# First FFN weights of block two rounded inside the attention loop, and one group of DRAM adds issued inside the attention's closing

## The chip, the cores and the metric

One core of one Trainium2 chip. The metric is the device time of one execution in microseconds; the kernel before took 1028.0 us (median of 3 runs, 1027.74 to 1028.08). PE is TensorE, DVE is VectorE, ACT is ScalarE, POOL is GpSimd, and SP is SyncE, which here only issues DMA.

## The reference

Two decoder blocks over 512 tokens of width 1024, in fp32: block one is a gated short convolution and a SwiGLU, block two is sliding-window attention with sinks and a SwiGLU.

```
for l in range(DEPTH):                        # DEPTH = 2
    if l < N_A:
        mix = short_conv_mixer(rmsnorm(h, ...), a_w_in[l], a_conv_w[l], a_w_out[l])
        h = h + rmsnorm(mix, a_post_norm[l])
    else:
        ...                                   # shared k, v; q; 16 heads, window 128, sinks
        attn = sliding_window_sink_attention(q, k_sh, v_sh, b_sinks[j]) @ b_w_o[j]
        h = h + rmsnorm(attn, b_post_norm[j])
    ff = swiglu(rmsnorm(h, ffn_pre_norm[l]), ffn_w_gate_up[l], ffn_w_down[l])
    h = h + rmsnorm(ff, ffn_post_norm[l])
```

The place of interest is the middle line of the second branch: the product with `b_w_o`, the norm behind it, and the first product of the SwiGLU that follows.

## The kernel before

Every fp32 operand is split into a high part, rounded to float32r, and a low part, the rest; a product is three matmuls (`mm3`). So each weight tile costs, beside its 512 KB fetch into one of seven `raw` buffers (SP queue, `fetch`), a rounding on ACT (`whi<-raw`) and a subtraction on DVE (`wlo<-raw,whi`). `Ahead` does this for the weights of the next stage: its constructor issues two fetches, and each `one()` rounds one 128x1024 tile, subtracts, and fetches the next.

The large products save multiplications by working with sums of weight blocks. These sums are formed in DRAM by DMA: `Sums` lists the copies and the accumulating transfers, `sum_on(at)` first issues all that is pending on the POOL queue and then makes the next step of every running group pending, and `issue(n)` issues pending ones. A group with four sums has four steps: four copies (`ab`, `ac`, `abc`, `abcd`), then `ab += b` and `ac += c`, then `abc += ab`, then `abcd += abc`. A transfer whose source or destination another transfer is still writing waits on the POOL engine's queue, and what stands behind it there waits too.

The attention loop runs `i` from 0 to 9 (`KT + 2` passes). `ORDER` is the order of one pass, written by hand; each letter is a step for a pair of heads `t` that depends on `i`. In pass 8 only the tail of the last pair, t = 7, is left: its probabilities are transposed (T, tile `pt`), split into `phi` on ACT (P) and `plo` on DVE (L), for the last block into `lp`, and multiplied with the values (W, tile `po`). Beside this, pass 8 holds the last two early units of the output projection (Z into `pe`, copied out by z into `mixo`) and the rounding of the last `w_o` tile (G). Pass 9 holds O, which splits `po` into `ohi` and `olo`.

Then comes `close`, for four token tiles t = 0 to 3 of two halves each. PE multiplies into `pmix`; for each half DVE adds (`take`, `mixo<-pmix,mixo`, L259) and ACT squares with a sum (`square_mix`, L264); then, for the tile, DVE adds up the sums (`mean`, `uv`, L293), POOL raises to the power -0.5 (`ur`, L297), DVE updates `h` (L302), ACT squares `h` (L310), DVE and POOL form the second factor (`mean2`: L315, L319), and ACT writes the normed tile (`norm`, `xn`, L324). In the middle of the last half tile (3, 1) PE transposes `xn` of tiles 0 and 1 (`turn`, tile `xt`, L335). Behind it, `ffn(1)` begins with `last_tile` and `project_first` (tile `pgu`). The first half tiles of `close` are begun in two parts of nine matmuls each, with two `ahead.one()` behind each part.

On PE, DVE, ACT and POOL the order of the instructions is that of the code (`manual_schedule`); on SP the scheduler orders the transfers.

Of the kernel before, what the change touches and what calls it, by code (L numbers as in the profile page):

```python
# [19 lines left out]
KT = D // P  # L20
# [24 lines left out]

EARLY_IN, REST_IN = 2, 0
ORDER = (
    "R- T0 g0 S0 O- T1 Q0 M0 Q1 Z0 P0 P1 S1 T2 L0 Q2 L1 G M1 E00 E01 T3 H- Q3 P2 P3 E10 E11 Z1 z0 K W0 L2 L3 N0 W1 W2 N1 W3 g1 z1"
)
STEP = {  # L50
    "S": "scores", "M": "maxima", "E": "exponents", "N": "normalise", "T": "turn", "P": "high",
# [4 lines left out]
EARLY = 4  # L56
# [8 lines left out]
G_FPRE = (24, 32)  # L65
# [3 lines left out]
B_CONV, B_ATT, B_FFN = 0, 1, (2, 3)  # L69
# [3 lines left out]
def yoco_kernel(  # L73
# [54 lines left out]
    def bank(s, pool=None):  # L128

        if pool is None:  # L130
            pool = (ps_mm, ps_sc, ps_mm, ps_pt)[turn[0] % 4]
            turn[0] += 1
        return pool.tile([P, S], F32, tag="bank", name=name(s))
# [69 lines left out]
    def unit(ps, t, ws, x, ks, n, k0=0, c0=0, c1=S):  # L203

        tk = slice(t * P, (t + 1) * P)
        for k in ks:
            w = ws[k // 2]
            kk = slice((k % 2) * S + c0, (k % 2) * S + c1)
            mm3(ps, x[k0 + k][0][:, tk], x[k0 + k][1][:, tk], w[0][:, kk], w[1][:, kk],
                k == 0, k == n - 1)  # L210
# [313 lines left out]
    issues = []  # L524

    def issue(n, behind=None):

        for dst, src, op in issues[:n]:
            if len(dst.shape) == 3:
                dst, src = (t.rearrange("k (a b) c -> (k a) (b c)", b=4) for t in (dst, src))  # L530
            else:
                dst, src = (t.rearrange("(a b) c -> a (b c)", b=2) for t in (dst, src))
            kw = {} if op is None else {"accum_op": op}
            made = tc.keep_in_program_order(
                nc.gpsimd.dma_start(dst, src, max_dma_last_dim=4 * 4 * S, **kw))  # L535
            if behind is not None:
                tc.add_manual_dep(
                    made.ins, behind.ins.name, mybir.DependencyInfo(
                        mybir.DependencyClass.Sync, mybir.DependencyReason.DATA),
                    reason="pace")  # L540
        del issues[:n]
# [13 lines left out]
    def sum_on(at):  # L555

        issue(len(issues))
        if at in BEGIN:
            summing.append(sums_of[BEGIN[at]])
        for x in summing:  # L560
            x.step()
        summing[:] = [x for x in summing if x.steps]
# [164 lines left out]
    res = Update(mix_c, B_CONV, [G_FPRE[0]])  # L727
# [116 lines left out]
    def tile_done(res, t, square=True):  # L844

        if t > 0:
            res.mean2(t - 1)
        res.scale(t, 0)
        res.mean(t)
        if t > 0:  # L850
            res.norm(t - 1)
        res.scale(t, 1)
        res.update(t)
        if square:
            res.square(t)

    def close(ws, x, k0, res, ahead, then=None):


        n = len(x) - k0  # L860

        def part(ps, t, half, ks):
            unit(ps, t, ws[len(ws) // 2 * half :], x, ks, n, k0)

        begun = [bank("pmix", ps_mm) for _ in range(2)]
        for half in range(2):
            part(begun[half], 0, half, range(n - 1))
            ahead.one()
            ahead.one()
        for t in range(NB):  # L870
            for half in range(2):
                if t == 0:
                    ps = begun[half]
                    part(ps, t, half, range(n - 1, n))
                else:
                    ps = bank("pmix", ps_mm)
                    if (t, half) == (NB - 1, 1):
                        part(ps, t, half, range(2))
                        for b in range(4):
                            res.turn(b, (0, 1))  # L880
                        part(ps, t, half, range(2, n))
                        for f in range(4):
                            res.split(0, f, 0)
                        res.square_mix(t, 0)
                        res.square(NB - 2)
                        res.scale(t, 0)
                    else:
                        part(ps, t, half, range(n))
                res.take(t, half, ps)
                if (t, half) != (NB - 1, 0):  # L890
                    res.square_mix(t, half)
            if t < NB - 1:
                tile_done(res, t, square=t < NB - 2)
            if t == 0 and then:
                then()
# [40 lines left out]
    def first_weights(l):  # L936
        return ([w_gu[l, f, j] for f in range(2) for j in range(2)]
                + [w_gb[l, 0, b] for b in range(2)])
# [3 lines left out]
    ahead = Ahead(first_weights(0))  # L942
    with tc.manual_schedule(engines=ALL):

        def sums_on():
            sum_on("o1")
            issue(len(issues))

        close(ws, ys, 0, res, ahead, sums_on)


    def ffn(l, before, ahead, gain, gpres, following):
# [199 lines left out]
        if gpres:  # L1152
            ahead = Ahead(following)
            with tc.manual_schedule(engines=ALL):
                close(ws, acts[-1], 0, res, ahead)
            return res, ahead
# [29 lines left out]
    res, ahead = ffn(0, res, ahead, B_FFN[0], [G_KV, G_BPRE], [  # L1186
        w_k[0], w_k[1], w_v[:, 0:D], w_v[:, D:], w_q[0], w_q[1]])
# [21 lines left out]
    def rope(ps, eng):  # L1209
        sh = slot("sh")  # L1210
        nc.vector.stream_shuffle(sh, ps, swap)
        a = slot("ra")
        nc.vector.tensor_tensor(out=a, in0=ps, in1=ctab, op=ALU.mult)
        eng.tensor_tensor(out=sh, in0=sh, in1=stab, op=ALU.mult)
        eng.tensor_tensor(out=a, in0=a, in1=sh, op=ALU.add)
        return a

    def rope_split(a, eng):
        hi, lo = slot("rhi", F32R), slot("rlo", F32R)
        nc.scalar.activation(hi, a, AF.Copy)  # L1220
        eng.tensor_tensor(out=lo, in0=a, in1=hi.bitcast(F32), op=ALU.subtract)
        return hi, lo
# [162 lines left out]
    mix_o = [None] * NB  # L1385
    early_w, rest_w = [], []
# [3 lines left out]
    at = []  # L1390

    with tc.manual_schedule(engines=ALL):
        last_tile(res, [[(0, 4)], [(0, 5)], [], [(0, 6), (0, 7), (1, 0), (1, 1)],
                        [(1, f) for f in (4, 5, 2, 3, 6, 7)]])
        for hf in range(2):
            c = slice(hf * 256, (hf + 1) * 256)
# [48 lines left out]
    with tc.manual_schedule(engines=ALL):  # L1445
        sum_on("a0")
        for i in range(KT + 2):
            for c in ORDER.split():
                if c == "K":
                    if i == 2:  # L1450
                        ks.append(rope_split(rope(pk[1], nc.gpsimd), nc.gpsimd))
                    continue
                late = c.endswith("-")
                op, n = c[0], [int(d) for d in c[1:].rstrip("-")]
                t = i - late
                if op == "g":

                    u = 2 * (t - EARLY - 1) + n[0]
                    if u in (-2, -1, 2, 3):
                        j = u + 2 if u < 0 else u  # L1460
                        early_w.append(split_weights(w_o[j // 2, j % 2], slots=j >= EARLY_IN))
                    continue
                if op in "SMENTPLWO":
                    t -= op in "TPLWO"
                    of = hp
                elif op in "QRH":
                    t += LEAD
                    of = qs
                elif op == "G":
                    t += LEAD + 1  # L1470
                    of = qs
                    if KT <= t < KT + 4:
                        j = t - KT
                        rest_w.append(split_weights(w_o[j // 2, 2 + j % 2], slots=j >= REST_IN))
                else:
                    t = 2 * (t - EARLY - 1) + n.pop(0)
                    of = early
                if 0 <= t < len(of) and not (op in "RH" and t < LEAD - 1):
                    getattr(of[t], STEP[op])(*n)
                if op in "RH":  # L1480
                    issue(len(issues) // 2 if op == "R" else len(issues))
            sum_on(f"a{i + 1}")

        res = Update(mix_o, B_ATT, [G_FPRE[1]])
        res.leaves = True
        res.load()
        ahead = Ahead(first_weights(1))
        close(rest_w, at, EARLY, res, ahead)
    ffn(1, res, ahead, B_FFN[1], [], [])


# [93 lines left out]
```

## Time and profile before

| | |
|---|---|
| median of 3 runs | 1028.0 us (1027.74 to 1028.08) |
| the profiled execution: its time | 1032.36 us |
| the profiled execution: its span | 1030.6 us |
| granted TensorE clock, mean over the span | 0.997 |
| busy: DVE | 823.2 us (80%) |
| busy: ACT | 577.7 us (56%) |
| busy: POOL | 195.3 us (19%) |
| the attention's pass 8 and 9 | about 651 to 662 us of the span |
| the closing behind the attention | about 661.5 to 690 us |

The profiled execution is 4.4 us longer than the median of the others, so a difference between two kernels is taken between figures of the same kind. Times in the profile are microseconds from the start of the span. A timeline row gives start, duration, engine, line, operation, the tile written and those read, the count, and in square brackets how long the engine had been idle before it and what ended that. Successive instructions of an engine overlap somewhat, so the pitch of a chain (start to start) is shorter than the duration of one. For a DMA row on POOL the duration is that of the issue; the time until the data has landed is given in the view of the DMA issues.

### The profile page before, as it was taken

To read this page: it belongs to the slowest core of one execution; us is meant where nothing else is said; L and a number is where in the kernel's file an instruction comes from. 1 tells how busy PE (TensorE), PEld (TensorE's weight loads), DVE (VectorE), ACT (ScalarE), POOL (GpSimd) and SP (SyncE) were. 2 spreads that over 40 slices of the span, in tenths; PEclk is the share of its full clock that TensorE was granted. 3 is DMA by queue.
4 is the path that set the end of the run, shared out by engine and by line. 5 is a ranking of instruction groups with operands and counts; after the bars stand their busy time and mean duration, and the time that the engine had idled before them with its cause. 6 is when DMAs were issued, how large, how long until landed. Compare 5 with 4: busy or idle time off the path is not lost.

```text
span 1030.6 us, 17465 instructions
## 1 busy us (share of the span) xinstructions
PE 1019.1 (99%) x6648; PEld 927.8 (90%) x6648; DVE 823.2 (80%) x1400; ACT 577.7 (56%) x1035; POOL 195.3 (19%) x259
## 2 busy tenths in 40 slices
PE   9999999999999999999999999989999999999997
PEld 8888888999899898998897888879998999989986
DVE  5766767888688879779869999668886788887786
ACT  7323445865655354656566677667565554645642
POOL 0333033111111111000124653121111010210001
PEclk9999999999999999999999999999999999999999
DMA  9897689459968699778404789865889676988732
GB/s 355 284 261 229 184 254 353 130 169 299 351 229 293 194 314 332 242 232 296 146 21 149 190 273 254 248 223 158 261 287 328 176 252 203 312 296 251 246 136 82
DMA packets 66580, 244.59 MB, mean 237 GB/s; under 512 B 7872, under 2 KB 8384, under 8 KB 54720
## 3 DMA queue, kind: packets, MB, share of 16 engines
q1 hardware_dynamic: 51328, 145.98, 38.4%
q0 software_dynamic: 14592, 96.48, 36.4%
q8 instruction: 52, 0.85, 0.3%
q10 hardware_dynamic: 576, 1.02, 0.3%
q14 instruction: 32, 0.26, 0.1%
HBM read 237.15 MB, written 102.76 MB: 330 GB/s over the span
## 4 chain that ended last, share of the span: by engine, by line
PE 90%; DVE 4%; DMA 3%; ACT 1%; issue 1%; POOL 1%; DVEq 0%; ACTq 0%
PE gx L193 7%; PE gx L192 7%; PE gx L191 7%; PE gz L193 4%; PE gz L192 4%; PE gz L191 4%; PE pcub L192 4%; PE pcub L193 4%; PE pcub L191 4%; PE px L191 4%; PE px L192 4%; PE px L193 4%; PE pmix L192 2%; PE pmix L191 2%; PE pmix L193 2%; DMA hsum<-in_w_gb_dram 2%
## 5 line engine op out<-in xcount | busy, mean ns | idle before, releaser
L467 DVE TENSOR_TENSOR wlo<-raw,whi 128x1024 fp32r<-128x1024 f32 x225 | 275.2, 1227 | 93.3 <-ACT whi L466 93.2
L466 ACT ACTIVATE whi<-raw 128x1024 fp32r<-128x1024 f32 x225 | 234.2, 1049 | 117.5 <-DVE raw L454 20.4
L191 PE MATMUL gx<-xt,whi 128*128 128x256 f32 x480 | 135.8, 283 | 0.0
L192 PE MATMUL gx<-xt,whi 128*128 128x256 f32 x480 | 135.8, 283 | 0.0
L193 PE MATMUL gx<-xt,wlo 128*128 128x256 f32 x480 | 135.8, 283 | 0.0
L191 PEld LDWEIGHTS gx<-xt,whi 128*128 128x128 f32 x480 | 92.2, 192 | 0.0
L192 PEld LDWEIGHTS gx<-xt,whi 128*128 128x128 f32 x480 | 92.2, 192 | 0.0
L193 PEld LDWEIGHTS gx<-xt,wlo 128*128 128x128 f32 x480 | 92.2, 192 | 0.0
L535 POOL DMA_DIRECT2D hsum<-in_w_gb_dram x96 | 63.4, 747 | 143.7 <-ACT whi L466 82.2
L1001 ACT ACTIVATE st<-gx 128x256 f32<-128x256 f32 x80 | 30.6, 385 | 83.5 <-PE gx L193 83.5
L535 POOL DMA_DIRECT2D hsum<-hsum x32 | 25.3, 790 | 262.4 <-ACT whi L466 208.6
L192 PE MATMUL pcub<-xhi,whi 128*128 128x512 f32 x168 | 65.4, 389 | 0.0
L191 PE MATMUL pcub<-xlo,whi 128*128 128x512 f32 x168 | 65.4, 389 | 0.0
L193 PE MATMUL pcub<-xhi,wlo 128*128 128x512 f32 x168 | 65.4, 389 | 0.0
L191 PE MATMUL px<-wlo,ahi 128*128 128x512 f32 x120 | 46.7, 389 | 0.0
L192 PE MATMUL px<-whi,ahi 128*128 128x512 f32 x120 | 46.7, 389 | 0.0
L193 PE MATMUL px<-whi,alo 128*128 128x512 f32 x120 | 46.7, 389 | 0.0
L193 PE MATMUL gx<-xhi,wlo 128*128 128x256 f32 x160 | 45.3, 283 | 0.0
L191 PE MATMUL gy<-xlo,whi 128*128 128x256 f32 x160 | 45.3, 283 | 0.0
L192 PE MATMUL gy<-xhi,whi 128*128 128x256 f32 x160 | 45.3, 283 | 0.0
L193 PE MATMUL gy<-xhi,wlo 128*128 128x256 f32 x160 | 45.3, 283 | 0.0
L191 PE MATMUL gz<-xt,whi 128*128 128x256 f32 x160 | 45.3, 283 | 0.0
(268 smaller groups left out, 3122.5 us busy)
## 6 DMA issues: line engine op xcount, KB each, us to landing
hsum<-in_w_gb_dram POOLq DMA_DIRECT2D x96, 512.0 KB, 7.9
raw<-hsum SPq DMA_DIRECT2D x88, 512.0 KB, 8.2
raw<-in_w_gb_dram SPq DMA_DIRECT2D x60, 512.0 KB, 7.4
hsum<-in_w_dn_dram POOLq DMA_DIRECT2D x36, 512.0 KB, 8.3
raw<-in_w_dn_dram SPq DMA_DIRECT2D x32, 512.0 KB, 7.3
hsum<-hsum POOLq DMA_DIRECT2D x28, 512.0 KB, 5.6
raw<-in_w_in_dram SPq DMA_DIRECT2D x21, 512.0 KB, 7.6
hsum<-in_w_dn_dram POOLq DMA_DIRECT2D x12, 768.0 KB, 12.6
```

Source lines behind the costliest of these rows:

```text
L191: nc.tensor.matmul(out, whi, xlo, start=start, stop=False, **kw)
L192: nc.tensor.matmul(out, whi, xhi, start=False, stop=False, **kw)
L193: nc.tensor.matmul(out, wlo, xhi, start=False, stop=stop, **kw)
L466: self.begun = nc.scalar.activation(hi[:, :n], raw, AF.Copy)
L467: nc.vector.tensor_tensor(out=lo[:, :n], in0=raw, in1=hi[:, :n].bitcast(F32), op=ALU.subtract)
L535: nc.gpsimd.dma_start(dst, src, max_dma_last_dim=4 * 4 * S, **kw))
L1001: nc.scalar.activation(s, x, AF.Copy)
```

## The change

The constructor of the closing's `Update` and of `Ahead` move to the start of pass 8; four steps A are written into `ORDER`, and in pass 8 each is one `ahead.one()`; in `close` the four calls fall away where `ahead` is `None`. The load of the gain vector (`res.load`) moves to the start of pass 9, still ahead of its use. The last `sum_on` of the loop moves from the end of pass 9 to behind the first tile of `close`, and there what it makes pending is issued at once.

```diff
 ORDER = (
-    "R- T0 g0 S0 O- T1 Q0 M0 Q1 Z0 P0 P1 S1 T2 L0 Q2 L1 G M1 E00 E01 T3 H- Q3 P2 P3 E10 E11 Z1 z0 K W0 L2 L3 N0 W1 W2 N1 W3 g1 z1"
+    "R- T0 g0 S0 O- T1 Q0 M0 Q1 Z0 P0 P1 S1 T2 L0 Q2 L1 G A M1 E00 E01 T3 H- Q3 P2 P3 A E10 E11 Z1 z0 K W0 L2 L3 A N0 W1 W2 N1 W3 g1 z1 A"
 )
...
         for half in range(2):
             part(begun[half], 0, half, range(n - 1))
-            ahead.one()
-            ahead.one()
+            if ahead:
+                ahead.one()
+                ahead.one()
...
         for i in range(KT + 2):
+            if i == KT:
+                res = Update(mix_o, B_ATT, [G_FPRE[1]])
+                res.leaves = True
+                ahead = Ahead(first_weights(1))
+            if i == KT + 1:
+                res.load()
             for c in ORDER.split():
+                if c == "A":
+                    if i == KT:
+                        ahead.one()
+                    continue
...
-            sum_on(f"a{i + 1}")
-
-        res = Update(mix_o, B_ATT, [G_FPRE[1]])
-        res.leaves = True
-        res.load()
-        ahead = Ahead(first_weights(1))
-        close(rest_w, at, EARLY, res, ahead)
+            if i < KT + 1:
+                sum_on(f"a{i + 1}")
+
+        def sums_on():
+            sum_on(f"a{KT + 2}")
+            issue(len(issues))
+
+        close(rest_w, at, EARLY, res, None, sums_on)
     ffn(1, res, ahead, B_FFN[1], [], [])
```

No instruction is added or removed. PE's order does not change. On SP the fetch of the last `w_o` tile moves behind the first two fetches of the gate and up weights.

ACT, pass 8 to the closing, before (L180 is the last `w_o` tile, L408 the first FFN weights, 5859 the last transposed block):

```order
L180 ACTIVATE whi_7438<-raw_7435 128x512
L1343 ACTIVATE phi_7431<-pt_7426 128x512
L1343 ACTIVATE lp_5859<-pt_7445 128x2x128
L1382 ACTIVATE mixo_7159<-pe_7411 128x512
L1382 ACTIVATE mixo_7212<-pe_7453 128x512
L1364 ACTIVATE ohi_7496<-po_7467 128x512
L408 ACTIVATE whi_7522<-raw_7507 128x1024
```

and now:

```order
L180 ACTIVATE whi_7445<-raw_7442 128x512
L408 ACTIVATE whi_7452<-raw_7393 128x1024
L1344 ACTIVATE phi_7438<-pt_7433 128x512
L1344 ACTIVATE lp_5859<-pt_7458 128x2x128
L408 ACTIVATE whi_7466<-raw_7395 128x1024
L1383 ACTIVATE mixo_7159<-pe_7418 128x512
L408 ACTIVATE whi_7495<-raw_7456 128x1024
L1383 ACTIVATE mixo_7212<-pe_7472 128x512
L408 ACTIVATE whi_7520<-raw_7470 128x1024
L1365 ACTIVATE ohi_7530<-po_7486 128x512
```

The four roundings, which stood in a row behind `ohi`, now stand between the steps of pass 8; one is ahead of the last `phi`.

DVE at the same place, before (L181 is the last `w_o` tile, L413 the first FFN weights):

```order
L181 TENSOR_TENSOR wlo_7440<-raw_7435,whi_7438 128x512
L1347 TENSOR_TENSOR plo_7432<-pt_7426,phi_7431 128x512
L1347 TENSOR_TENSOR lp_5860<-pt_7445,lp_5859 128x2x128
L1365 TENSOR_TENSOR olo_7497<-po_7467,ohi_7496 128x512
L413 TENSOR_TENSOR wlo_7523<-raw_7507,whi_7522 128x1024
```

and now:

```order
L181 TENSOR_TENSOR wlo_7447<-raw_7442,whi_7445 128x512
L413 TENSOR_TENSOR wlo_7453<-raw_7393,whi_7452 128x1024
L413 TENSOR_TENSOR wlo_7467<-raw_7395,whi_7466 128x1024
L1348 TENSOR_TENSOR plo_7439<-pt_7433,phi_7438 128x512
L1348 TENSOR_TENSOR lp_5860<-pt_7458,lp_5859 128x2x128
L413 TENSOR_TENSOR wlo_7496<-raw_7456,whi_7495 128x1024
L413 TENSOR_TENSOR wlo_7521<-raw_7470,whi_7520 128x1024
L1366 TENSOR_TENSOR olo_7531<-po_7486,ohi_7530 128x512
```

Two of the subtractions stand ahead of the last `plo` and `lp`, and two ahead of `olo`.

POOL, the end of pass 9 and the start of the closing, before (`hsum_208` to `hsum_211` are `ab`, `ac`, `abc` and `abcd` of the group of down weights that was begun last):

```order
L535 DMA hsum_211<-in_w_dn_dram 64x2048
L535 DMA hsum_208<-in_w_dn_dram 64x2048
L535 DMA hsum_209<-in_w_dn_dram 64x2048
L297 TENSOR_TENSOR ur_7503<-uv_7502,mhalf 128x1
L319 TENSOR_TENSOR ur_7503<-uv_7502,mhalf 128x1
L297 TENSOR_TENSOR ur_7503<-uv_7502,mhalf 128x1
```

and now:

```order
L535 DMA hsum_211<-in_w_dn_dram 64x2048
L535 DMA hsum_208<-in_w_dn_dram 64x2048
L535 DMA hsum_209<-in_w_dn_dram 64x2048
L297 TENSOR_TENSOR ur_7392<-uv_7391,mhalf 128x1
L535 DMA hsum_210<-hsum_208 64x2048
L319 TENSOR_TENSOR ur_7392<-uv_7391,mhalf 128x1
L297 TENSOR_TENSOR ur_7392<-uv_7391,mhalf 128x1
```

The transfer `abc += ab` (`hsum_210<-hsum_208`), which stood behind the eighth and last `ur` of the closing, now stands behind the first; what reads `hsum_208` there is written by the second row.

## The prediction

> **What bounds the kernel now.** I read the page's first part, then the waits of PE, then the timeline of each engine from pass 8 to the end of the closing. First the page's line of busy time and PE's waits over the whole span (what waited, for what: us in total, times, longest):
>
> ```profile
> PE 1019.1 (99%) x6648; PEld 927.8 (90%) x6648; DVE 823.2 (80%) x1400; ACT 577.7 (56%) x1035; POOL 195.3 (19%) x259
> ...
> PE xt L335 <- ACT xn L324: 2.7, 1, 2.7
> PE idle L663 <- DVE ones L140: 1.1, 1, 1.1
> PE psc L1273 <- DVE nm L1285: 0.6, 2, 0.3
> ```
>
> PE is the bound nearly everywhere. Of other engines it waits once for 2.7 us, in the very stage that the change touches, and otherwise for 1.7 us in all. No later wait can swallow a delay of PE, so a microsecond that PE gains or loses here reaches the end. Next PE around that wait, and the stretches behind it (bounds; then busy time and count of PE, PEld, DVE, ACT, POOL; granted clock; DMA share; GB/s):
>
> ```profile
> 681.72 0.39 PE L193 MATMUL pmix<-whi,olo 128*128 128x512 f32 x1
> 681.95 0.27 PE L335 MATMUL xt<-ident,xn 128*128 128x128 f32 x1
> 684.90 2.39 PE L335 MATMUL xt<-ident,xn 128*128 128x128 f32 x15 [2.69 <-ACT xn L324]
> ...
> 687.94 0.63 PE L193 MATMUL pmix<-whi,olo 128*128 128x512 f32 x1
> 688.37 0.63 PE L191 MATMUL pmix<-wlo,ohi 128*128 128x512 f32 x1
> ...
> 685.00:687.00 2.00, 2.00 (x16) 2.00 (x16) 1.90 (x3) 1.39 (x3) 0.06 (x1) 0.77 0.11 41
> 687.00:689.00 2.00, 2.00 (x7) 1.61 (x6) 2.00 (x5) 1.64 (x4) 0.00 (x0) 0.50 0.67 270
> 689.00:690.00 1.00, 1.00 (x6) 0.86 (x6) 0.37 (x2) 0.59 (x2) 0.00 (x0) 0.76 0.00 0
> ```
>
> PE needs the normed tile 1 at about 682.2 and gets it at 684.9. The granted clock then falls to 0.50: a matmul of 512 columns goes from a pitch of 0.23 us (681.72 to 681.95) to 0.43. From the three shares, half speed lasts 0.9 + 2.0 + 0.5 = 3.4 us and costs 1.7. So the wait is worth 2.7 + 1.7 = 4.4 us, the most that the change could bring.
>
> Why is tile 1 late? POOL in the closing, with the last transfers ahead of it, and the updates of `h` on DVE:
>
> ```profile
> 659.93 2.29 POOL L535 DMA_DIRECT2D hsum<-in_w_dn_dram  x4
> 671.22 0.80 POOL L535 DMA_DIRECT2D hsum<-in_w_dn_dram  x1 [9.00 <-DMA hsum<-in_w_dn_dram]
> 673.02 0.79 POOL L535 DMA_DIRECT2D hsum<-in_w_dn_dram  x1 [1.00 <-DMA hsum<-in_w_dn_dram]
> 673.56 0.85 POOL L297 TENSOR_TENSOR ur<-uv,mhalf 128x1 f32<-128x1 f32 x1
> 677.24 0.56 POOL L319 TENSOR_TENSOR ur<-uv,mhalf 128x1 f32<-128x1 f32 x1 [2.83 <-DVE uv L315]
> 678.81 0.93 POOL L297 TENSOR_TENSOR ur<-uv,mhalf 128x1 f32<-128x1 f32 x1 [1.02 <-DVE uv L293]
> ...
> 670.08 0.21 DVE L293 TENSOR_SCALAR uv<-us 128x1 f32<-128x1 f32 x1
> 674.45 1.28 DVE L302 SCALAR_TENSOR_TENSOR h<-mixo,ur,h 128x1024 f32<-128x1024 f32 x1 [3.56 <-POOL ur L297]
> 679.77 1.28 DVE L302 SCALAR_TENSOR_TENSOR h<-mixo,ur,h 128x1024 f32<-128x1024 f32 x1 [0.44 <-POOL ur L297]
> ```
>
> DVE has tile 0's sum ready at 670.3; POOL takes it up at 673.56, since two accumulating transfers ahead of it in its queue wait for the copies into `hsum_208` and `hsum_209` (9.00 and 1.00 us). That is 3.3 us of delay, carried from tile to tile: tile 1's update starts at 679.77, and its transposes 5.13 us later.
>
> **The roundings.** Four tiles leave the closing and enter pass 8. Their data are there (the four fetches are issued at 611.14 to 633.7, below; with the swap on SP the first two go one place earlier and the last `w_o` tile goes third, still some 30 us ahead of its use at 653), so moving the fetches costs nothing. The rows that time the rest:
>
> ```profile
> 611.14 22.59 SPq L160 DMA_DIRECT2D raw<-in_w_gu_dram  x4
> ...
> 656.07 0.63 ACT L180 ACTIVATE whi<-raw 128x512 fp32r<-128x512 f32 x1 [2.29 <-PE pt L1330]
> 656.61 0.58 ACT L1343 ACTIVATE phi<-pt 128x512 fp32r<-128x512 f32 x1
> 657.08 0.38 ACT L1343 ACTIVATE lp<-pt 128x256 fp32r<-128x256 f32 x1
> 657.35 0.60 ACT L1382 ACTIVATE mixo<-pe 128x512 f32<-128x512 f32 x1
> 662.21 3.89 ACT L408 ACTIVATE whi<-raw 128x1024 fp32r<-128x1024 f32 x4
> ...
> 657.34 0.68 DVE L1347 TENSOR_TENSOR plo<-pt,phi 128x512 fp32r<-128x512 f32 x1
> 663.30 4.63 DVE L413 TENSOR_TENSOR wlo<-raw,whi 128x1024 fp32r<-128x1024 f32 x4 [0.26 <-ACT whi L408]
> 667.85 0.68 DVE L259 TENSOR_TENSOR mixo<-pmix,mixo 128x512 f32<-128x512 f32 x1
> ...
> 660.07 0.28 PE L191 MATMUL po<-plo,vt 128*128 128x256 f32 x1
> ```
>
> A rounding has a pitch of 0.97 us on ACT (3.89 / 4), a subtraction 1.16 on DVE (4.63 / 4). ACT: first rounding 656.6, `phi` 657.6, `lp` 658.05, second rounding 658.3 to 659.4. DVE stands on the second subtraction until 659.4 + 1.16 = 660.6, and only then does the last `plo`, which ended at 658.0 before; now 661.3. PE wants it at 660.07: **a new wait of 1.2 to 1.3 us** that the kernel before did not have. The two later roundings delay `ohi` and `olo` to about 664.6; the begun half tiles need `olo` only after 18 matmuls (18 x 0.23 = 4.1 us from 662.8), so nothing.
>
> In the closing the first `take` ran at 667.85, right behind the subtractions, when PE had been ready about 1.4 us. Now DVE is free, but PE comes 1.3 us later: 661.5 + 1.3 + 21 x 0.23 and the end of the last matmul give 667.8 again. **The removal brings nothing to the chain**; and even had it brought 1.4 us, POOL would not take the sum before 673.6. The 1.3 us of PE are not lost beside the rest either: PE now reaches the transposes at 683.5 and waits there anyway.
>
> **The transfer put behind the first tile.** `hsum_210<-hsum_208` reads what the transfer issued at 671.22 writes. From the view of the DMA issues, for narrow windows (KB, us from issue to landing), the transfers issued at 671.22 and 673.02, the add at 658.19, a copy at 634.86; and an older transfer of the same kind on POOL:
>
> ```profile
> hsum<-in_w_dn_dram POOLq DMA_DIRECT2D x1, 512.0 KB, 10.0
> hsum<-in_w_dn_dram POOLq DMA_DIRECT2D x1, 512.0 KB, 11.3
> hsum<-in_w_gb_dram POOLq DMA_DIRECT2D x1, 512.0 KB, 8.1
> hsum<-in_w_gb_dram POOLq DMA_DIRECT2D x1, 512.0 KB, 7.2
> ...
> 639.15 0.84 POOL L535 DMA_DIRECT2D hsum<-hsum  x1 [3.22 <-DMA hsum<-hsum]
> ```
>
> The last row shows such a transfer holding POOL until its source has landed. So POOL stands from 674.1 until 671.22 + 10.0 = 681.2. Queued behind it are the `ur` for tile 0's norm (677.24 before) and, the one that matters, tile 1's (678.81), for which DVE's update waits, and behind that update the takes of tile 2. With 0.3 us from landing to issue (copy, 11.0 after 659.93, against 671.22), 0.54 to the next POOL step (673.02 to 673.56), 0.55 for L319 and 0.96 from L297 to the update (678.81 to 679.77): 681.2 + 2.35 = 683.55, **3.8 us later than 679.77**. The transposes follow at 683.55 + 5.13 = 688.7. PE waits there 5.2 us instead of 2.7, and its end moves by 1.3 + 2.5 = 3.8.
>
> Is 681.2 still right? SP's five fetches for the FFN wait for the raw buffers, hence for the subtractions:
>
> ```profile
> 657.45 9.69 SPq L437 DMA_DIRECT2D raw<-hsum  x4
> 667.96 0.33 SPq L437 DMA_DIRECT2D raw<-in_w_gb_dram  x1
> ...
> 655.00:660.00 5.00, 5.00 (x32) 4.39 (x31) 2.32 (x4) 2.48 (x5) 1.40 (x3) 1.00 0.54 202
> 660.00:665.00 5.00, 5.00 (x30) 4.39 (x30) 2.39 (x3) 3.29 (x4) 2.22 (x5) 1.00 0.89 150
> ```
>
> They now go at about 658.9 to 664.0: the first 1.5 us later, the others 4 us earlier. The bytes that compete with the copies and the add are nearly the same; the fetches press on the copies sooner and are gone sooner. I keep 681.2. Bounds: a copy of 7.2 us and an add of 8.1 give 659.93 + 7.2 + 8.1 = 675.2, where nothing waits; a copy slowed by 2 and an add of 11.3 give 684.8, which is 3.6 more.
>
> **The clock.** Before, full speed was back 4.6 us after the restart (689.5), with 1.2 us of these at full. After a wait twice as long I take all 4.6 us at half speed: 2.3 lost instead of 1.7, so +0.6, bounds 0 and +1.7 (as much again). [...]
>
> **Sum**: 3.8 + 0.6 = 4.4. The profiled execution (1032.36; span 1030.6) would become 1036.8; the median 1028.0 becomes **1032.4 us**.
>
> **Rivals.** *A: the add lands soon enough.* Up to a landing at 677.4 the update of tile 1 is not delayed. For it: quieter DMA from 670 on, as the fetches are gone. Against it: adds of 8.1 to 11.3 us, and the issue at 671.2 hangs on copies that now compete more. Landing at 678 gives +0.6 for the update, perhaps +0.3 of clock: 1028.9.
>
> *B: faster.* The copies land in 7.2 us and release the adds at 667.4; then POOL is free for tile 0 at 670.3, its update runs 3.3 us earlier, and the add lands by 667.4 + 8.1 = 675.5, so tile 1's update starts at 677.9 (+ 2.35, as above) and its transposes could at 683.0, before PE's 683.5. The one wait is gone with its clock loss, the 1.3 us stay: 1028.0 - 4.4 + 1.3 = 1024.9. It decides where the copies land under about 8 us, 3 less than before. For it: the fetches that crowded 664.5 to 675 start earlier, and the DMA share is 0.54 just ahead. Against it: 11.0 us measured while fewer fetches competed. [...] This trace has 7.2 to 11.3 for one, which is why B stays unlikely.
>
> *C: worse.* Copies held back by the earlier fetches, an add of 11.3 us: landing 684.8, 4.4 + 3.6 = 8.0 and more with the clock: 1036.
>
> *D: the roundings alone count*, that is, the moved transfer does not hold POOL. Then 1.3 us of new wait only shortens the old one, as xn still comes at 684.9: 1028.0. The row at 639.15 speaks against it; I count it with A.
>
> **How the numbers follow.** Forecast 0.68, A (with D) 0.14, B 0.09, C 0.09. What can be told from no change here is 0.2%, 2.06 us. Forecast and C are slower by more; of A nearly all, and a quarter of B, are within; the rest of B is faster: faster 0.07, same 0.14, slower 0.79. The forecast's own range is 1030.3 to 1035; the range for 8 in 10 reaches down into A and up to C, 1028.0 to 1036.0.
>
> **What would show it.** In the trace after: an idle time of POOL of some 7 us ahead of a `hsum<-hsum` that stands between the first and the second `ur` of the closing; tile 1's update near 683.5; PE's wait on `xn` near 5 us, with the clock at 0.50 behind it; a wait of PE on `plo` of about 1.3 us near 660; the first `take` still near 667.8. I am wrong if the moved transfer finds its source landed, or if the copies ahead of the closing come much sooner.

## The result, and the profile after

The kernel takes 1033.83 us (median of 12 runs, 1030.75 to 1036.42); the kernel before took 1027.95 us on the same chip (median of 12). The ratio is 1.0055, with a 95% interval of 1.0042 to 1.0068: slower by 0.55%, some 5.9 us. The profiled execution took 1032.08 us, with a span of 1030.3 us; it is the slowest of the four fastest runs.

PE's waits over the whole span (what waited, for what: us in total, times, longest):

```profile
PE xt L335 <- ACT xn L324: 3.2, 1, 3.2
PE idle L663 <- DVE ones L140: 1.1, 1, 1.1
PE po L191 <- DVE plo L1348: 1.0, 1, 1.0
```

The one wait of before has become longer, and a new one stands in pass 8. POOL's timeline at the place of the moved transfer:

```profile
658.62 2.29 POOL L535 DMA_DIRECT2D hsum<-in_w_dn_dram  x4
669.89 0.80 POOL L535 DMA_DIRECT2D hsum<-in_w_dn_dram  x1 [8.98 <-DMA hsum<-in_w_dn_dram]
671.76 0.79 POOL L535 DMA_DIRECT2D hsum<-in_w_dn_dram  x1 [1.07 <-DMA hsum<-in_w_dn_dram]
672.30 0.85 POOL L297 TENSOR_TENSOR ur<-uv,mhalf 128x1 f32<-128x1 f32 x1
679.11 0.82 POOL L535 DMA_DIRECT2D hsum<-hsum  x1 [5.96 <-issue]
679.70 0.84 POOL L319 TENSOR_TENSOR ur<-uv,mhalf 128x1 f32<-128x1 f32 x1
680.23 0.82 POOL L297 TENSOR_TENSOR ur<-uv,mhalf 128x1 f32<-128x1 f32 x1
```

Behind the first `ur` POOL stands idle for 5.96 us; then the transfer goes out, and the two `ur` that had been queued behind it follow at once. The profile names "issue" as the releaser, that is, nothing that it shows; it is the landing of the add issued at 669.89, which by the view of the DMA issues took 8.7 us, to 678.6. DVE at the two places of interest:

```profile
658.93 1.23 DVE L413 TENSOR_TENSOR wlo<-raw,whi 128x1024 fp32r<-128x1024 f32 x1 [0.47 <-ACT whi L408]
660.07 0.68 DVE L1348 TENSOR_TENSOR plo<-pt,phi 128x512 fp32r<-128x512 f32 x1
...
667.33 1.37 DVE L259 TENSOR_TENSOR mixo<-pmix,mixo 128x512 f32<-128x512 f32 x2 [3.37 <-PE pmix L193]
...
673.19 1.28 DVE L302 SCALAR_TENSOR_TENSOR h<-mixo,ur,h 128x1024 f32<-128x1024 f32 x1 [2.81 <-POOL ur L297]
...
681.09 1.28 DVE L302 SCALAR_TENSOR_TENSOR h<-mixo,ur,h 128x1024 f32<-128x1024 f32 x1 [3.01 <-POOL ur L297]
```

The second subtraction holds back the last `plo`. In the closing the first `take` now finds DVE idle for 3.37 us, waiting for PE: the freed engine gains nothing. Tile 1's update waits 3.01 us for POOL. PE at both waits, and two stretches behind the second (granted clock in the third place from the end):

```profile
660.81 0.39 PE L191 MATMUL po<-plo,vt 128*128 128x256 f32 x1 [1.03 <-DVE plo L1348]
...
682.77 0.27 PE L335 MATMUL xt<-ident,xn 128*128 128x128 f32 x1
686.22 1.86 PE L335 MATMUL xt<-ident,xn 128*128 128x128 f32 x15 [3.17 <-ACT xn L324]
```

```profile
686.00:688.00 2.00, 1.78 (x16) 1.79 (x17) 1.59 (x2) 1.36 (x4) 0.38 (x1) 1.00 0.08 23
688.00:690.00 2.00, 2.00 (x14) 1.75 (x12) 2.00 (x6) 1.97 (x5) 0.00 (x0) 1.00 0.65 268
```

In this execution the clock stayed at 1.00 behind a wait of 3.17 us. By the mean clock of its runs this is luck: four runs with 0.998 lie at 1030.75 to 1032.08, three with 0.996 or 0.997 at 1033.09 to 1034.31, and five with 0.995 at 1035.68 to 1036.42. The other runs have no profile, only a mean clock; that it fell at this place is argued from the executions below that have one, and not shown.

### The profile page after: what moved, and what is told of

Read it like the earlier page. It is cut to its first block, busy times and chain, and to the rows that moved or that the text cites. A ratio compares the mean times of both kernels' runs of the same rounds, so it can differ in the third digit from the quotient of the medians.

```text
span 1030.3 us, 17465 instructions
## 1 busy us (share of the span) xinstructions
PE 1017.2 (99%) x6648; PEld 926.0 (90%) x6648; DVE 823.5 (80%) x1400; ACT 578.2 (56%) x1035; POOL 195.1 (19%) x259
## 4 chain that ended last, share of the span: by engine, by line
PE 89%; DMA 4%; DVE 4%; issue 1%; ACT 1%; POOL 1%; DVEq 0%; SPq 0%; ACTq 0%
PE gx L193 7%; PE gx L192 7%; PE gx L191 7%; PE gz L193 4%; PE gz L192 4%; PE gz L191 4%; PE pcub L193 4%; PE pcub L191 4%; PE pcub L192 4%; PE px L191 4%; PE px L192 4%; PE px L193 4%; PE pmix L193 2%; PE pmix L192 2%; PE pmix L191 2%; DMA hsum<-in_w_gb_dram 2%
```

## The experiments

Theory: the moved transfer holds POOL until the add before it has landed, and that makes tile 1's normed tile late for PE; the roundings in pass 8 cost PE 1.0 us, which its later wait swallows. Rivals: the roundings are the cost; a transfer issued inside the closing costs by itself. The times of each run below stand beside those of the kernel before on the same occasion, and each run has the profile of one execution.

**The roundings alone.** From the changed kernel the last adds go back to their old place:

```diff
-            if i < KT + 1:
-                sum_on(f"a{i + 1}")
+            sum_on(f"a{i + 1}")
...
-        close(rest_w, at, EARLY, res, None, sums_on)
+        close(rest_w, at, EARLY, res, None)
```

> The change's roundings in pass 8, but the last adds issued where they were before (behind the closing's last ur). Theory (the moved add is the cost): the wait of PE on plo near 660 stays (about 1.0 us), the wait on xn is no longer than in the kernel before, median 1028.0 to 1029.2. Rival (the roundings in pass 8 are the cost): median near that of the change, 1033 to 1034.

Measured: 1029.76 us (12 runs) beside 1028.57, ratio 1.0015 (1.0002 to 1.0028). That is 0.6 us over the top of what was expected, as the kernel before is itself 0.6 us longer on this occasion than its 1027.95, and far from 1033. PE's waits in its profiled execution, its POOL, and its clock:

```profile
PE xt L335 <- ACT xn L324: 3.4, 1, 3.4
PE idle L663 <- DVE ones L140: 1.1, 1, 1.1
PE po L191 <- DVE plo L1348: 1.0, 1, 1.0
```

```profile
659.97 2.28 POOL L535 DMA_DIRECT2D hsum<-in_w_dn_dram  x4
673.44 0.80 POOL L535 DMA_DIRECT2D hsum<-in_w_dn_dram  x1 [11.19 <-DMA hsum<-in_w_dn_dram]
```

```profile
686.00:688.00 2.00, 0.88 (x4) 0.89 (x5) 1.50 (x3) 1.06 (x2) 0.93 (x1) 0.62 0.03 12
688.00:690.00 2.00, 2.00 (x12) 2.00 (x11) 1.98 (x4) 1.19 (x3) 0.00 (x0) 0.53 0.30 123
```

This execution took 1034.39 us, the slowest of the kernel's 12 runs, and no likeness of its median: here the copies happened to land late, POOL was held, and the wait on `xn` came without the moved transfer. Ten of the 12 runs lie between 1028.6 and 1030.6. So the roundings alone cost about 1.2 us (by the interval, 0.2 to 2.9). That is near the 1.0 us of the wait on `plo`, but that this wait is what the median pays is not shown: the run with the second rounding late, below, takes the wait away and its median gains nothing.

**The moved transfer alone.** The kernel before, with only the last `sum_on` moved:

```diff
-            sum_on(f"a{i + 1}")
+            if i < KT + 1:
+                sum_on(f"a{i + 1}")
...
-        close(rest_w, at, EARLY, res, ahead)
+        def sums_on():
+            sum_on(f"a{KT + 2}")
+            issue(len(issues))
+
+        close(rest_w, at, EARLY, res, ahead, sums_on)
```

> The kernel before, with only the last add moved behind the closing's first tile. Theory: POOL idles about 6 us ahead of hsum<-hsum behind the first ur, tile 1's update comes near 681 to 684, PE waits on xn 4 to 5 us (1 us more than in the change, as PE arrives 1 us earlier), median 1032.5 to 1035. Rival (roundings are the cost): median within 0.5 us of 1028.

Measured: 1033.73 us (8 runs), ratio 1.0047 (1.0031 to 1.0062), the whole cost of the change. POOL and the stretches behind PE's wait:

```profile
669.85 0.94 POOL L297 TENSOR_TENSOR ur<-uv,mhalf 128x1 f32<-128x1 f32 x1
677.13 0.82 POOL L535 DMA_DIRECT2D hsum<-hsum  x1 [6.33 <-issue]
677.72 0.84 POOL L319 TENSOR_TENSOR ur<-uv,mhalf 128x1 f32<-128x1 f32 x1
678.25 0.82 POOL L297 TENSOR_TENSOR ur<-uv,mhalf 128x1 f32<-128x1 f32 x1
```

```profile
684.00:686.00 2.00, 1.77 (x12) 1.77 (x13) 1.57 (x2) 1.09 (x3) 0.40 (x1) 0.78 0.66 254
686.00:688.00 2.00, 2.00 (x9) 1.71 (x8) 1.91 (x5) 1.55 (x4) 0.00 (x0) 0.50 0.65 268
688.00:690.00 2.00, 2.00 (x14) 1.82 (x13) 1.45 (x3) 1.25 (x4) 0.05 (x1) 0.86 0.03 8
```

The hold is there, 6.33 us. The update of tile 1 came at 679.1 and PE waited 2.52 us, both less than expected: in this, its fastest execution (1031.78), the copies landed early, and the first add went out at 667.56 where the change has 669.89.

**The moved transfer behind tile 1.** The change, with the place in `close` made an argument:

```diff
-            if t == 0 and then:
+            if t == when and then:
...
-        close(rest_w, at, EARLY, res, None, sums_on)
+        close(rest_w, at, EARLY, res, None, sums_on, 1)
```

> The change, with the add behind tile 1 in place of tile 0. Theory (what costs is the time until the source has landed, near 679 to 681): POOL reaches the transfer after tile 1's ur, waits under 2.5 us, no ur that matters is late, median 1028.0 to 1029.5. Rival (a transfer issued inside the closing costs by itself): median 1032 or more.

Measured: 1029.47 us (12 runs), ratio 1.0011 (0.9995 to 1.0027), as expected of the theory. POOL:

```profile
676.96 0.93 POOL L297 TENSOR_TENSOR ur<-uv,mhalf 128x1 f32<-128x1 f32 x1 [1.02 <-DVE uv L293]
679.09 0.82 POOL L535 DMA_DIRECT2D hsum<-hsum  x1 [1.20 <-issue]
```

The same transfer goes out at the same moment, 679.1, but behind the `ur` that matters; PE's wait on `xn` is 0.2 us here. In median this kernel is 0.9 us over the kernel before, the change 5.9: five us come back from one place in a queue. Four of the 12 runs are still above 1030.5, up to 1034.6.

**A transfer that waits for nothing.** The kernel before, with one copy of the next group's weights behind tile 0:

```diff
+        def copy_on():
+            dst, src, _ = sums_of["g15"].steps[0].pop(0)
+            issues.insert(0, (dst, src, None))
+            issue(1)
+
+        close(rest_w, at, EARLY, res, ahead, copy_on)
```

> The kernel before, with one copy of the next group of gate weights, whose source nobody writes, issued on POOL behind tile 0; the last add stays where it was before. Theory (the wait is the cost, not the issue): POOL is held under 1 us, median within 0.6 us of the kernel before. Rival (issue or traffic in the closing): 2 us or more above it.

Measured: 1027.71 us (12 runs), ratio 0.9991 (0.9981 to 1.0). POOL and PE's wait:

```profile
670.50 0.85 POOL L297 TENSOR_TENSOR ur<-uv,mhalf 128x1 f32<-128x1 f32 x1
671.02 0.82 POOL L535 DMA_DIRECT2D hsum<-in_w_gb_dram  x1
674.19 0.56 POOL L319 TENSOR_TENSOR ur<-uv,mhalf 128x1 f32<-128x1 f32 x1 [2.35 <-DVE uv L315]
```

```profile
PE xt L335 <- ACT xn L324: 0.3, 1, 0.3
```

The issue (0.82 us) and the traffic of this copy cost nothing that the median shows; the wait does (5.96 us of POOL and 5.9 us of median in the change). This profiled execution, 1027.77 us, also stands for the kernel before at its median, of which there is no profile: hardly any wait on `xn`.

**The wait doubled.** The change, with `abcd += abc` issued behind `abc += ab` at tile 0:

```diff
-            sum_on(f"a{KT + 2}")
-            issue(len(issues))
+            for step in range(2):
+                sum_on(f"a{KT + 2 + step}")
+                issue(len(issues))
```

> The change with the suspected wait doubled: behind tile 0 both abc += ab and abcd += abc, the second of which waits for the first. Theory: POOL is held some 8 us longer (a hsum<-hsum landed after 8.3 us before), tile 1's update near 689, PE's wait on xn near 11 us, median 1041 to 1044. Rival (a fixed cost of moving transfers, not the wait): 1034 to 1036.

Measured: 1042.77 us (4 runs, 1042.52 to 1046.53), ratio 1.0149 (1.0133 to 1.0166). POOL, and the update of tile 1:

```profile
678.54 0.82 POOL L535 DMA_DIRECT2D hsum<-hsum  x1 [5.67 <-issue]
686.92 0.77 POOL L535 DMA_DIRECT2D hsum<-hsum  x1 [7.55 <-issue]
```

```profile
688.84 1.28 DVE L302 SCALAR_TENSOR_TENSOR h<-mixo,ur,h 128x1024 f32<-128x1024 f32 x1 [11.04 <-POOL ur L297]
```

POOL is held 8.4 us longer (678.54 to 686.92), PE's two waits on `xn` add up to 10.3 us where near 11 were expected, and the kernel takes 8.9 us more than the change.

**The second rounding late.** The roundings of the change with the adds as before, and the second A moved behind `L3`, so that it no longer stands ahead of the last `plo`:

```diff
-... G A M1 E00 E01 T3 H- Q3 P2 P3 A E10 E11 Z1 z0 K W0 L2 L3 A N0 ...
+... G A M1 E00 E01 T3 H- Q3 P2 P3 E10 E11 Z1 z0 K W0 L2 L3 A A N0 ...
```

> The roundings of the change with the second one put behind the last block's plo and lp (so two stand there together), the last adds as before. Theory (the 1.0 us wait on plo comes from the second subtraction standing ahead of it): that wait is gone, median 0.8 to 1.2 us under the run with the roundings as the change has them (1029.8), so 1028.5 to 1029.1, and no better than the kernel before. Rival (pass 8 is slower for another reason): the wait goes but the median stays at 1029.5 or more. Second rival (freeing the closing of the roundings gains): 1027 or less.

Measured: 1029.58 us (12 runs), ratio 1.0025 (1.001 to 1.004). DVE and PE's wait:

```profile
657.69 1.23 DVE L413 TENSOR_TENSOR wlo<-raw,whi 128x1024 fp32r<-128x1024 f32 x1 [0.26 <-ACT whi L408]
658.84 0.68 DVE L1348 TENSOR_TENSOR plo<-pt,phi 128x512 fp32r<-128x512 f32 x1
```

```profile
PE xt L335 <- ACT xn L324: 1.4, 1, 1.4
```

The wait on `plo` is gone, but the median did not come down as expected: five of the 12 runs are between 1031.35 and 1034.28, the other seven between 1028.19 and 1029.62. With 1029.58 the rival's condition, 1029.5 or more, is met: pass 8 is slower for another reason than the wait on `plo`. That PE arrives earlier and meets POOL's hold more often is one such reason; it is argued, not shown. The same kernel once more:

> The kernel of the run with the roundings in pass 8, the second one late, once more: 5 of its 12 runs were above 1031, of the kernel before 11 of 72 above 1030.5. If the earlier fetches slow the copies that release POOL, again a third or more of the runs is above 1030.5; if it was chance, about one in seven.

Measured: 1028.77 us (12 runs), ratio 1.002 (1.0006 to 1.0034), four of 12 above 1030.5. This is the third or more that was expected if the earlier fetches slow the copies. Together 9 of 24, against 13 of the 95 runs of the kernel before on all these occasions; the roundings alone had 3 of 12. A reason may be in the fetches that the early subtractions let go: from the first copy's issue on POOL to the first add it takes 10.7 to 13.5 us in the seven profiles with the roundings in pass 8 and POOL's order as before up to there, and 9.9, 9.9 and 11.3 in the three without. That is one execution each, so it stays a likely reason and not a shown one.

**The change with the second rounding late.** The same move of the second A as just shown, with the transfer left behind tile 0: does PE's wait on `plo` matter beside the hold?

> The change with only the second rounding put behind the last plo and lp. Theory (the 1.0 us that PE loses there is swallowed by its wait on xn, which POOL's hold sets): no wait on plo, the wait on xn about 1 us longer, median within 1 us of the change (1033.8). Rival (the wait on plo adds up with the wait on xn): near 1032.8 or less in median, at an unchanged wait on xn.

Measured: 1032.94 us (5 runs, 1031.78 to 1034.84), ratio 1.0052 (1.004 to 1.0064). PE, and the stretches after it restarts:

```profile
681.70 0.33 PE L335 MATMUL xt<-ident,xn 128*128 128x128 f32 x1
686.14 3.46 PE L335 MATMUL xt<-ident,xn 128*128 128x128 f32 x15 [4.11 <-ACT xn L324]
```

```profile
684.00:686.00 2.00, 0.00 (x0) 0.00 (x0) 1.50 (x3) 1.97 (x5) 0.98 (x2) 0.83 0.70 262
686.00:688.00 2.00, 1.86 (x9) 1.87 (x10) 1.67 (x2) 0.62 (x3) 0.30 (x1) 0.50 0.06 20
688.00:690.00 2.00, 2.00 (x10) 1.90 (x9) 1.49 (x4) 1.24 (x3) 0.00 (x0) 0.50 0.64 266
690.00:692.00 2.00, 2.00 (x7) 1.52 (x6) 1.18 (x2) 1.87 (x5) 0.00 (x0) 0.50 0.03 8
692.00:694.00 2.00, 2.00 (x18) 2.00 (x17) 1.01 (x4) 1.02 (x3) 0.55 (x1) 0.96 0.00 0
```

PE's wait on `xn` is longer by the microsecond that it no longer waits on `plo` (4.11 against 3.17), and it restarts at the same time (686.14 against 686.22). With so few runs and such a spread in the clock, the median's 0.9 us under the change is not told from none.

**The adds behind the closing.** The kernel before, with the two adds that hold POOL ahead of the first tile sent behind the last:

```diff
-                if op in "RH":
+                if op in "RH" and i <= KT:
...
-            sum_on(f"a{i + 1}")
+            if i <= KT:
+                sum_on(f"a{i + 1}")
```

> The kernel before, with the two accumulating transfers that wait for their copies ahead of the closing moved behind its last ur, so POOL is free when the first sum is ready. Theory (POOL's hold is the only reason that xn is late): first ur near 670.5, PE waits on xn under 0.3 us in every run, clock 0.998 or more, median 1027.3 to 1028.2 and no run above 1029.5. Rival (the wait on xn has another source, DVE or ACT): single runs above 1031 stay.

Measured: 1027.67 us (11 runs, 1027.02 to 1028.82), ratio 0.9993 (0.9985 to 1.0002). The first `ur` no longer waits for a transfer:

```profile
669.86 0.94 POOL L297 TENSOR_TENSOR ur<-uv,mhalf 128x1 f32<-128x1 f32 x1 [8.86 <-DVE uv L293]
```

The median hardly moves; what goes is the tail. No run is above 1029, where the kernel before had 5 of 29 above 1030.5 on the same occasion; with the two runs that follow, none of 33 is above 1029.

**Both.** This, and the roundings in pass 8 with the second one late.

> Both of these: roundings in pass 8 with the second one late, and the two accumulating transfers behind the closing. Theory: no wait of PE on plo or xn; PE is the bound, so no gain over the free closing with the roundings in it: 1027.3 to 1028.3. Rival (the roundings in the closing still cost something once POOL is free): 0.5 us or more under it.

> The kernel with both the late second rounding and the two accumulating transfers behind the closing, once more: again 1027.2 to 1027.8 in median, no run above 1028.5, and 0 to 0.8 us under the kernel before.

Measured: 1027.46 us (11 runs, up to 1027.91), ratio 0.9989 (0.9979 to 0.9999); again 1027.34 us (11 runs, up to 1028.03), ratio 0.9994 (0.9985 to 1.0002). PE does not wait in the closing, and its 16 transposes stand in one row:

```profile
681.85 1.91 PE L335 MATMUL xt<-ident,xn 128*128 128x128 f32 x16
```

It is the fastest of all by median, but 0.2 to 0.3 us under the run without the roundings is within the spread. Once POOL is free, nothing is left in the closing for the roundings to bring.

## Why the prediction was right, point by point

- **The place and the mechanism** were right. The transfer holds POOL (5.96 us where 7 were forecast), tile 1's update is late, PE waits longer on `xn`. The four runs that move, keep, free or double the wait (1029.5, 1033.7, 1027.7, 1042.8 us) and the roundings alone (1029.8) settle it against a cost of the roundings and against a cost of the transfer itself.
- **The roundings**: forecast a wait on `plo` of 1.2 to 1.3 us, measured 1.03. That the later wait covers it is shown by PE's restart at the same time with and without it (686.22, 686.14). Where hardly any later wait does, in the profiled execution of the transfer behind tile 1, it is lost: 1028.98 less the waits of 1.0 and 0.2 us is 1027.8, the time of the kernel before. In the medians the two are not separated, as the late second rounding took this wait away and still cost 1.0 to 1.5 us. That the freed closing brings nothing was right: the first `take` waits for PE.
- **The landing of the add** was forecast at 681.2. It was issued 1.3 us sooner than before (669.89, not 671.22) and took 8.7 us where 10.0 were taken, so it landed at 678.6; POOL went on at 679.1, so tile 1's update came at 681.09 and not 683.55, and PE's wait was 3.17 us and not 5.2. The term of 3.8 us was too large as a difference from the profiled execution of before.
- **The base was wrong**, in the step that carried the sum of 4.4 over from the profiled execution (1032.36) to the median (1028.0) as if the 4.4 us between these two were the price of profiling. They were the wait and the clock themselves: 2.7 + 1.7. The profiled executions bear this out: less PE's waits on `xn` and `plo` and half of the time that PE ran at half speed, the kernel before comes to 1028.0, the change to 1027.9, the transfer alone to 1027.6, the roundings alone to 1028.5, the doubled wait to 1028.1 and the change with the late rounding to 1027.7. So the kernel before has no such wait at its median, and 13 of its 95 runs have times above 1030.5, like the profiled one's. Counted from the median the sum is 1027.95 + 1.0 + 3.2 = 1032.15, and the profiled execution after, at full clock, took 1032.08. Two errors, a wait forecast too long and a base with a wait in it, offset each other, and that is luck: counted from a median without a wait, the forecast's own terms (1.3 + 5.2 + 2.3) give 1036.8, the same as it gave for the profiled execution, which took 1032.08.
- **The clock** was a term of 0.6 us with a bound of 1.7, on top of the 1.7 us in the base. By time and mean clock the 12 runs after stand in three groups, with middles at 1031.5, 1033.4 and 1035.8. One stretch of half speed, 3.4 us, costs 1.7 us, and two up to 3.4, as an estimate from the stretches below; so the groups are likely those with none, one and two, and 1032.15 + 1.7 = 1033.85 is a median run with one. Only a run without a stretch was profiled, so this is argued; it also leaves some 1 us of the slowest group open.
- **The rivals**: B did not come true; its copies would have had to land in 8 us and took 11.3 to the next issue. Its mechanism did, in the run with the adds behind the closing, where it is worth 0.4 us in the median, which is not told from none, and the tail. A's time for the landing nearly came true (678.6, where it had 678 for 1028.9), and yet the kernel took 1033.8: like the forecast, A counted from a base with a wait in it. C's 1036 is met by five single runs; whether by a late landing, as C has it, or by the clock, no profile shows. D did not come true: POOL was held.

## What to carry to other kernels

A transfer that had to wait for another one's data was not work that an engine's queue did on the side: here it stopped POOL for 5.96 us behind the first `ur`, and its price was set by what was queued behind it (5.9 us over the kernel before there, 0.9 behind tile 1's `ur`), so look at the engine that issues it and put it behind the last instruction that a busy chain needs. Before a difference is worked out, ask whether the one execution that was profiled is like the median; when its time is 4 us off and it shows a wait of that worth, the wait may be the exception and not the thing to remove. And an engine that was freed ahead of a chain gained nothing here, as another engine set the chain's pace: DVE then stood idle for 3.37 us ahead of the first `take`, waiting for PE.

## What the runs showed of the hardware

Half speed came in multiples of one length, 3.4 us. Worked out from the granted clock in the windows, it lasted 3.4 us in the profiled execution before, 3.4 in the roundings alone (1.5 + 1.9), 3.4 in the transfer alone (0.9 + 2.0 + 0.6), 6.8 in the change with the late rounding (0.68 + 6.0 + 0.16), and 13.6 in the doubled wait (0.50 from 686 to 698, 0.60 from 698 to 700). A wait of 3.17 us in the changed kernel had none behind it, while those of 2.52 us (the transfer alone) and 2.69 us (the kernel before) had one stretch of 3.4 each. So it is not the length of the wait alone that decides; what else does was not shown. In these traces a wait of some 3 us cost from 3.2 us (the changed kernel) to 4.8 (the roundings alone, 3.4 and 1.4 of clock, as PE still stood idle for 0.6 us of that stretch), and the 12 runs of the changed kernel have mean clocks from 0.995 to 0.998; that two stretches behind such a wait make the top of the changed kernel's spread, 1030.75 to 1036.42, is likely and not shown.
